# The opening of a diffusion backbone on one core: where the small rows load, who squares, and in which order tiles are turned

## The chip, the core and the metric

The kernel runs on one core of a Trainium2 chip. The metric is device time in microseconds (us); lower is better. The kernel before takes 922.6 us, the median of three runs (922.02, 922.60, 925.86).

A core has engines that run side by side and wait for each other by semaphores: TensorE (PE) multiplies matrices and turns tiles, VectorE (DVE) and ScalarE (ACT) work element by element, GpSimd (POOL) does the same slowly and starts loads, SyncE (SP) starts loads. PSUM is the memory that TensorE writes; its banks hold 128 x 512 floats each here.

## What is computed

One layer of a backbone on 512 latent tokens x and 256 context tokens, width 1024. The opening computes the modulation from c and the normed, modulated input, and starts the first products with `w_in`:

```
sh1x, sc1x, ... = split(silu(c) @ w_ada + b_ada, 6)       # for c and for c_ctx
hx = rms_norm(x, norm1_g) * (1 + sc1x) + sh1x
z = hx @ w_in                                              # 512 x 7200
u, vs, q, r, ga, gb, k, v, lr = split(z)
a = spatial_gating(gelu(u), gelu(vs))
o = gated linear attention over q, k, v, decay from lr, states started by the context tokens
y = (sigmoid(ga) * (a @ w_br_a) + sigmoid(gb) * (silu(r) * norm(o) @ w_br_b)) @ w_o
x = x + g1x * y
x = x + g2x * conv_glu(modulate(rms_norm(x, norm2_g)))
out = rms_norm(x, final_norm_g)
```

Products are taken in three parts: each operand is split in a high part (float32r, rounded) and a low part (the rest), and high*high, high*low and low*high are summed.

## The kernel before

x lies in four token tiles of 128 tokens, each in two halves of 512 columns (`xin[t][0]`, `xin[t][1]`). What the opening does, by line of the kernel before:

- POOL makes the identity, ones and two triangular masks (L105 to L117). ACT starts four small loads, `rows_a` (L127): c, c_ctx, norm1_g (8 rows of 128 each) and b_ada (48 rows), and `w_lr` (L314). POOL starts a second set of small rows and `w2r` (L350 to L357).
- SyncE starts the loads of x (eight of 256 KB, L134), then the ada weights in six groups (`ada_load`, L324) with the first weights of v, q and k between them (`first_load`, L330 and L333). These loads keep the order of the code. The framework gives each load started by SyncE or ACT one of eight lanes in turn; a load waits until the load before it on its lane has landed. Loads of POOL have lanes of their own.
- TensorE turns `rows_a` to columns (`columns`, L515, into `vec_a`), runs ten warm-up products of ones (L608; the trace shows each as two passes), then turns x: per tile seven blocks of 128 columns into seven banks (`xps`, L592).
- `norm_tiles` walks the tiles one at a time: ACT squares both halves with a sum (L546), small steps on VectorE and ACT make the root (L550 to L560), VectorE scales the tile (L563, L567; ACT scales the second half of the last one, L565), then `x_turns` turns it. Ahead of the last tile's turns stand the first ada dot (`ada_dot(0)`, L631: 32 small products), its copy by VectorE (L602) and its selection (`ada_sel`, L640, with three small steps on VectorE, L643 to L645).
- `ada_mod(0)` (L652) modulates the first block from its bank on ACT, VectorE casts the high part (L379) and takes the low part (L380). `first_high(0)` casts the first weights on ACT (L614), `x_out` copies the turned blocks out of their banks (L597). The eighth block is turned into a bank of the pool `mm` after that (`ps7`).
- The first products (`first_step`, L708) run over eight blocks k in three parts z, for q, k and four tiles of v (six products a part). The next ada group's dot, selection and modulation stand between them. The four v products use the four banks of the pool `mm`, so each waits until one is copied out.

TensorE, ACT and VectorE keep the order in which the code is recorded (`in_order` from `STRICT` on); what is recorded ahead of `STRICT` is ordered by the framework.

Of the kernel before, what the change touches and what calls it, by code (L numbers as in the profile page):

```python
# [11 lines left out]
U32 = mybir.dt.uint32  # L12
# [21 lines left out]
def backbone_kernel(  # L34
# [63 lines left out]
    def table_for(func):  # L98
# [9 lines left out]
    maskf = const([P, P], "maskf")  # L108
    G.affine_select(out=maskf, in_=ones, pattern=[[1, P]], base=0, channel_multiplier=-1,
                    compare_op=ALU.is_ge, fill=0.0)  # L110
    maskb = const([P, P], "maskb")
    G.affine_select(out=maskb, in_=ones, pattern=[[-1, P]], base=0, channel_multiplier=1,
                    compare_op=ALU.is_ge, fill=0.0)
# [4 lines left out]
    masks = (maskf.bitcast(U32), maskb.bitcast(U32))  # L118


# [5 lines left out]
    for o, ap in ((0, c[0]), (8, c_ctx), (16, norm1_g[0]), (24, b_ada[0])):  # L126
        adma(rows_a[o:o + ap.shape[0] // P, :], r8(ap))  # L127
# [186 lines left out]
    adma(w_lr, wi[:, O_LR:O_LR + 32].rearrange("(k p) c -> p k c", p=P))  # L314
# [13 lines left out]
    def first_load(i):  # L328
        rows = lambda c0, n: wi[2 * i * P:(2 * i + 2) * P, c0:c0 + n].rearrange("(k p) c -> p k c", p=P)
        dma(fv[i][0], rows(O_V, 512))  # L330
        raw = heap([P, 2, 2, P], s="qkraw")
        for j, c0 in enumerate((O_Q, O_K)):
            dma(raw[:, j], rows(c0, P))  # L333
        fqk.append((raw, late([P, 2, 2, P], F32R, s="qkh"), late([P, 2, 2, P], F32R, s="qkl")))
# [7 lines left out]
    was[4] = ada_load(4)  # L342
    first_load(2)
# [7 lines left out]
    G.dma_start(rows_b[32:40, :], gla_b2[0].rearrange("d (h p) -> (d h) p", p=P))  # L351
    w2r = []
# [160 lines left out]
    def columns(rows, n, name, bank=mm):  # L513
# [3 lines left out]
        V.tensor_copy(cols_, ps[:, :n])  # L517
        return cols_

    vec_a = columns(rows_a, 72, "vec_a")  # L520
    cT, n1g, bada = vec_a[:, 0:16], vec_a[:, 16:24], vec_a[:, 24:72]
    sg = small(16, "sg")
    A.activation(sg, cT, AF.Exp, scale=-1.0)
    V.tensor_scalar(sg, sg, 1.0, None, op0=ALU.add)
    V.reciprocal(sg, sg)
    cs = const([P, KT, 32], "cs")
    V.memset(cs, 0.0)
    V.tensor_tensor(cs[:, :, 0], cT[:, 0:8], sg[:, 0:8], op=ALU.mult)
    V.tensor_tensor(cs[:, :, 1], cT[:, 8:16], sg[:, 8:16], op=ALU.mult)
# [5 lines left out]
    bsc1 = const([P, 8], "bsc1")  # L535
    V.tensor_scalar(bsc1, bada[:, 8:16], 1.0, None, op0=ALU.add)
# [51 lines left out]
    STRICT = len(traced())  # L588
    xps = [(mm, gl)[k < 1 or k > 4]() for k in range(KT - 1)]
# [8 lines left out]

    def x_turns(t):
        if t == 3:  # L600
            dot0.extend(ada_dot(0))
            V.tensor_copy(*dot0)  # L602
            ada_sel(0, dot0[0])
# [1332 lines left out]
```

## Time and profile before

| | us |
|---|---|
| median of three runs | 922.6 |
| profiled execution, its own time | 921.73 |
| its span (first to last instruction) | 919.7 |
| VectorE, ACT and POOL busy in the span | 755.4, 484.7, 62.8 |
| TensorE busy from 0 to 22 us | 15.31 |
| loads started by SyncE, share of 16 DMA engines over the span | 41.0% |

The sums below are made against the profiled execution, which is 0.9 us faster than the median. In a row of the timeline stand the start, the duration, the engine, the line, the operation, the tile written and the tiles read, and in brackets how long the engine was idle before and what ended that. A row of stretches has the start and end, then the length, then busy time and number of instructions of PE, PEld (weight loads of TensorE), DVE, ACT and POOL, the granted clock, the DMA share and GB/s.

### The profile page before, as it was taken

What the parts mean: (1) busy time and instruction counts of PE and PEld (TensorE: products, weight loads), DVE (VectorE), ACT (ScalarE), POOL (GpSimd) and SP (SyncE); (2) the same over time, 40 slices, a digit from 0 to 9 for tenths busy, and PEclk for the clock granted to TensorE, in tenths of its full rate; (3) what the DMA queues carried; (4) which work ended last, traced back from release to release, by engine and by line L of the source; (5) the groups of instructions that cost most, each with busy time, mean ns of one, the idle gap of its engine ahead of it and who ended that gap; (6) DMA issues with size and microseconds to landing.
All of it is one profiled execution on the core that took longest, in us unless ns stands there. A gap on an engine that the chain in (4) does not pass through costs nothing.

```text
span 919.7 us, 12868 instructions
## 1 busy us (share of the span) xinstructions
PE 899.5 (98%) x4671; PEld 756.4 (82%) x4671; DVE 755.4 (82%) x1307; ACT 484.7 (53%) x869; POOL 62.8 (7%) x98
## 2 busy tenths in 40 slices
PE   7999999999999999999999998999999999999996
PEld 5777899988888888888888888988888888888885
DVE  5667686779589877978776887899998888899896
ACT  5156464657466447566552568543333443356673
POOL 3000000000000011113011010000000000122100
PEclk9999999999999999999999999999999999999998
DMA  9950512142088375978578164264444333399532
GB/s 275 338 159 1 154 31 59 34 115 70 15 279 306 97 202 124 288 171 219 160 206 206 33 175 138 69 178 131 126 131 133 104 91 115 79 231 260 151 92 92
DMA packets 125821, 134.27 MB, mean 146 GB/s; under 512 B 7178, under 2 KB 84310, under 8 KB 125758
## 3 DMA queue, kind: packets, MB, share of 16 engines
q1 hardware_dynamic: 115357, 116.80, 41.0%
q0 software_dynamic: 8672, 15.43, 10.3%
q10 hardware_dynamic: 1728, 1.22, 0.4%
q8 instruction: 37, 0.61, 0.3%
q14 instruction: 27, 0.21, 0.1%
HBM read 131.32 MB, written 2.10 MB: 145 GB/s over the span
## 4 chain that ended last, share of the span: by engine, by line
PE 89%; DVE 6%; ACT 2%; issue 1%; DMA 1%; ACTq 0%; DVEq 0%
PE mm L387 31%; PE mm L418 11%; PE gl L465 7%; PE gl L1719 6%; PE mm L465 5%; PE mm L1719 4%; PE gl L418 4%; PE gl L935 3%; PE mm L402 3%; PE mm L708 2%; PE mm L411 2%; PE gl L708 1%; PE mm L1041 1%; DVE mx L902 1%; PE gl L631 1%
## 5 line engine op out<-in xcount | busy, mean ns | idle before, releaser
L149 ACT CAST wh<-raw 128x1024 fp32r<-128x1024 f32 x110 | 115.0, 1050 | 113.4 <-PE mm L387 73.1
L150 DVE TENSOR_TENSOR wl<-raw,wh 128x1024 fp32r<-128x1024 f32 x110 | 133.6, 1220 | 34.2 <-ACT wh L149 31.7
L1602 DVE SCALAR_TENSOR_TENSOR cacc<-ca,ccol,cacc 128x441 f32<-128x441 f32 (+2 forms) x176 | 121.0, 693 | 6.7 <-ACT cacc L1590 3.6
L387 PE MATMUL mm<-h2l,wh 128*128 128x512 f32 x320 | 124.5, 389 | 0.0
L387 PE MATMUL mm<-h2h,wl 128*128 128x512 f32 x320 | 124.5, 389 | 0.0
L387 PE MATMUL mm<-h2h,wh 128*128 128x512 f32 x320 | 124.5, 389 | 0.0
L387 PEld LDWEIGHTS mm<-h2h,wl 128*128 128x128 f32 x320 | 60.1, 188 | 12.6
L387 PEld LDWEIGHTS mm<-h2l,wh 128*128 128x128 f32 x320 | 60.1, 188 | 12.5
L387 PEld LDWEIGHTS mm<-h2h,wh 128*128 128x128 f32 x320 | 60.1, 188 | 12.4
L1190 DVE SCALAR_TENSOR_TENSOR acc<-wa,cs,acc 128x512 f32<-128x512 f32 x64 | 45.8, 747 | 3.4 <-DMA wa<-in_w_ada_dram 3.4
L1605 ACT ACTIVATE cacc<-cacc 128x512 f32<-128x512 f32 x22 | 13.9, 632 | 60.6 <-DVE cacc L1602 60.5
L387 PE MATMUL mm<-hxh,wh 128*128 128x512 f32 x104 | 41.7, 401 | 0.0
L387 PE MATMUL mm<-hxh,wl 128*128 128x512 f32 x104 | 40.9, 394 | 0.0
L387 PE MATMUL mm<-hxl,wh 128*128 128x512 f32 x104 | 40.5, 390 | 0.0
L223 ACT CAST wh<-tt 128x512 fp32r<-128x512 f32 x48 | 28.3, 621 | 20.4 <-DMA tt<-in_w_in_dram 7.5
L224 DVE TENSOR_TENSOR wl<-tt,wh 128x512 fp32r<-128x512 f32 x48 | 31.6, 687 | 7.9 <-ACT wh L223 7.8
L1661 ACT CAST wh<-raw 128x1024 fp32r<-128x1024 f32 x22 | 23.0, 1052 | 18.2 <-PE mm L1719 9.0
L199 POOL DMA_DIRECT2D tt<-in_w_in_dram x24 | 20.8, 1064 | 165.5 <-DVE xl L1291 71.8
L1662 DVE TENSOR_TENSOR wl<-raw,wh 128x1024 fp32r<-128x1024 f32 x22 | 26.9, 1223 | 2.6 <-ACT wh L1661 2.6
L1641 POOL DMA_DIRECT2D b<-in_ffn_w_down_dram x11 | 9.4, 865 | 276.8 <-DMA b<-in_ffn_w_down_dram 268.3
L465 PE MATMUL mm<-wh,hxh 128*128 128x512 f32 x72 | 28.0, 389 | 0.0
L465 PE MATMUL mm<-wl,hxh 128*128 128x512 f32 x72 | 28.0, 389 | 0.0
(527 smaller groups left out, 2449.9 us busy)
## 6 DMA issues: line engine op xcount, KB each, us to landing
raw<-in_w_in_dram SPq DMA_DIRECT2D x54, 512.0 KB, 4.6
wa<-in_w_ada_dram SPq DMA_DIRECT2D x96, 256.0 KB, 5.0
raw<-in_ffn_w_up_dram SPq DMA_DIRECT2D x44, 512.0 KB, 3.9
raw<-in_ffn_w_down_dram SPq DMA_DIRECT2D x22, 512.0 KB, 3.3
tt<-in_w_in_dram POOLq DMA_DIRECT2D x24, 256.0 KB, 6.5
raw<-in_w_br_a_dram SPq DMA_DIRECT2D x8, 512.0 KB, 5.2
raw<-in_w_br_b_dram SPq DMA_DIRECT2D x8, 512.0 KB, 3.8
raw<-in_w_o_dram SPq DMA_DIRECT2D x8, 512.0 KB, 6.0
```

The lines of the kernel that those rows point to most:

```text
L149: A.copy(wh, raw)
L150: V.tensor_tensor(wl, raw, wh.bitcast(F32), op=ALU.subtract)
L223: A.copy(wh[:, kk, :], tt[j][kk])
L224: V.tensor_tensor(wl[:, kk, :], tt[j][kk], wh[:, kk, :].bitcast(F32), op=ALU.subtract)
L387: T.matmul(ps, a[:, k, :], b[:, c0:c0 + n], start=(k == 0 and i == 0), stop=(k == KT - 1 and i == 2))
L402: T.matmul(pss[u], a[:, k, :], b[:, c0:c0 + n], start=(k == 0 and z == 0), stop=(k == KT - 1 and z == 2))
L418: T.matmul(ps, a, b[:, k % 2, :], start=(k == 0 and i == 0), stop=(k == KT - 1 and i == 2))
L465: T.matmul(ps[t], a, b[:, kk, :], start=(first and i == 0), stop=(j == 1 and kk == 1 and i == 2), skip_group_check=again)
L708: T.matmul(fps[i], a, b, start=(k == 0 and z == 0), stop=(k == KT - 1 and z == 2))
L1190: V.scalar_tensor_tensor(a_, w_, cs[:, k, 0:1], a_, op0=ALU.mult, op1=ALU.add)
L1602: V.scalar_tensor_tensor(o, a_[:, r0 + dy:r1 + dy, c0 + dx:c1 + dx], wcol(tap), o, op0=ALU.mult, op1=ALU.add)
L1719: T.matmul(ps, a[:, t * P:(t + 1) * P], w[b][:, j, c0:c0 + n], start=(first and i == 0), stop=(last and i == 2), skip_group_check=again)
```

## The change

It touches the opening alone.

1. The four small loads of `rows_a` are started by POOL instead of ACT, ahead of the two masks. `w_lr` is loaded by SyncE, behind the fifth ada group. In `first_load` the q and k columns go ahead of the v columns.
2. `vec_a` is turned into a bank of the other pool (`gl`), and its copy is recorded later, behind the first root.
3. The squares of a tile's first half run on ACT, those of the second half on VectorE (`x_sq`). One root is taken for two tiles (`x_root`, `x_root_end`). First halves are scaled by VectorE (`x_low`), second halves by ACT (`x_high`).
4. Tiles 0 and 1 are turned whole, then the first four blocks of tiles 2 and 3, then the first ada dot, then the last three blocks of tiles 2 and 3, then the selection.
5. The scale `am` is made in one step with a column `bsn` prepared earlier. For the first block ACT writes the high part straight from the bank, and VectorE the full value from the bank and then the low part.
6. The eighth block is turned in the first products (k = 0, ahead of part z = 2) into a bank of `gl`. The cast of the first q and k weights stands ahead of the first modulation, that of v behind it and one copy.

```diff
-        adma(rows_a[o:o + ap.shape[0] // P, :], r8(ap))
+        G.dma_start(rows_a[o:o + ap.shape[0] // P, :], r8(ap))
...
-    adma(w_lr, wi[:, O_LR:O_LR + 32].rearrange("(k p) c -> p k c", p=P))
...
     was[4] = ada_load(4)
+    dma(w_lr, wi[:, O_LR:O_LR + 32].rearrange("(k p) c -> p k c", p=P))
...
-        V.tensor_tensor(am[:, ks, :], sv[:, :, 1, :], bsc1[:, ks].unsqueeze(2).to_broadcast([P, ng, 2]), op=ALU.add)
-        V.tensor_tensor(am[:, ks, :], am[:, ks, :], n1g[:, ks].unsqueeze(2).to_broadcast([P, ng, 2]), op=ALU.mult)
+        for b in range(ng):
+            k = k0 + b
+            V.scalar_tensor_tensor(am[:, k, :], sv[:, b, 1, :], n1g[:, k:k + 1],
+                                   bsn[:, k:k + 1].to_broadcast([P, 2]), op0=ALU.mult, op1=ALU.add)
...
-                A.activation(f, xps[0], AF.Identity, bias=bm_[:, 0, 0:1], scale=am[:, 0, 0:1])
+                A.activation(hi, xps[0], AF.Identity, bias=bm_[:, 0, 0:1], scale=am[:, 0, 0:1])
+                V.tensor_scalar(f, xps[0], am[:, 0, 0:1], bm_[:, 0, 0:1], op0=ALU.mult, op1=ALU.add)
+                V.tensor_tensor(lo, f, hi.bitcast(F32), op=ALU.subtract)
...
+    def x_sq(t, ss):
+        for hf in range(2):
+            junk = heap([P, 512], BF16, s="junk")
+            if hf == 0:
+                A.activation(junk, xin[t][0], AF.Square, accum_out=ss[:, t % 2:t % 2 + 1])
+            else:
+                V.scalar_tensor_tensor(junk, xin[t][1], 1.0, xin[t][1], op0=ALU.mult, op1=ALU.mult,
+                                       accum_out=ss[:, 2 + t % 2:3 + t % 2])
...
+    for t in range(2):
+        x_sq(t, ssx[0])
+    root0 = x_root(ssx[0])
+    x_root_end(*root0)
+    vec_copy[0]()
+    A.activation(sg, cT, AF.Exp, scale=-1.0)
+    for t in range(2):
+        x_low(t, root0[1])
+    x_sq(2, ssx[1])
+    x_high(0, root0[1])
...
+    x_sq(3, ssx[1])
+    x_high(1, root0[1])
+    root1 = x_root(ssx[1])
...
+    for t in range(2):
+        for k in range(KT - 1):
+            x_turn(xps[k], t, k)
+    for t in range(2, 4):
+        for k in range(4):
+            x_turn(xps[k], t, k)
     x_out(1, xps[1], V.tensor_copy)
+    dst, aps = ada_dot(0)
+    V.tensor_copy(dst, aps)
+    for t in range(2, 4):
+        for k in range(4, KT - 1):
+            x_turn(xps[k], t, k)
+    ada_sel(0, dst)
+    A.copy(*fqk[0][1::-1])
     ada_mod(0)
...
+            if k == 0 and z == 2:
+                ps7 = gl()
+                for t in range(4):
+                    x_turn(ps7, t, KT - 1)
+                x_out(KT - 1, ps7, A.copy)
```

Three places in the order of instructions. First POOL's queue at its start; `rows_92` and `rows_88` are `rows_a` before and after, `rows_223` and `rows_219` the second set. Before, POOL goes from the identity to the masks and then to the second set (`rows_a` is in ACT's queue):

```order
masks.py:199 AFFINE_SELECT ident<-ident 128x128
L109 AFFINE_SELECT maskf<-ones 128x128
L112 AFFINE_SELECT maskb<-ones 128x128
L115 MEMSET eps_t 128x1
L117 MEMSET one_t 128x1
L350 DMA rows_223<-in_norm_g_dram 8x128
L350 DMA rows_223<-in_sgu_ln_g_dram 8x128
```

And now:

```order
masks.py:199 AFFINE_SELECT ident<-ident 128x128
L109 MEMSET eps_t 128x1
L111 MEMSET one_t 128x1
L118 DMA rows_88<-in_c_dram 8x128
L118 DMA rows_88<-in_c_ctx_dram 8x128
L118 DMA rows_88<-in_norm_g_dram 8x128
L118 DMA rows_88<-in_b_ada_dram 48x128
L344 AFFINE_SELECT maskf<-ones 128x128
L347 AFFINE_SELECT maskb<-ones 128x128
L341 DMA rows_219<-in_norm_g_dram 8x128
```

The four small loads stand in POOL's queue where the masks stood, and b_ada is the last of them as before.

Second, ACT between the scaling of the last x tile and the first copies; `xT` are turned blocks, `qkh` and `wh` the high parts of the first weights. Before:

```order
L565 ACTIVATE xin_110<-xin_110,r_363 128x512
L652 ACTIVATE xT_270<-gl_263,bm,am 128x512
L614 CAST qkh_139<-qkraw_136 128x512
L614 CAST wh_114<-raw_113 128x1024
L597 COPY xT_273<-mm_266 128x512
L597 COPY xT_274<-mm_267 128x512
L597 COPY xT_277<-mm_425 128x512
```

And now:

```order
L772 ACTIVATE xin_102<-xin_102,r_107_325 128x512
L772 ACTIVATE xin_106<-xin_106,r_107_325 128x512
L811 CAST qkh_134<-qkraw_130 128x512
L645 ACTIVATE hxh_393<-gl_257,bm,am 128x512
L595 COPY xT_267<-mm_260 128x512
L815 CAST wh_110<-raw_109 128x1024
L595 COPY xT_268<-mm_261 128x512
```

The cast of the q and k weights moved ahead of the modulation, which now writes the high part `hxh`; the copy of the eighth block (`xT_277` from `mm_425`) is gone from this stretch.

Third, TensorE behind the first block's dot. The eighth block's turns (into `mm_425` before, `gl_453` now) read `xin`; `gl_436` and `gl_407` are the bank of q. Before:

```order
L592 MATMUL gl_269<-ident,xin_110 128x128
L592 MATMUL mm_425<-ident,xin_98 128x128
L592 MATMUL mm_425<-ident,xin_102 128x128
L592 MATMUL mm_425<-ident,xin_106 128x128
L592 MATMUL mm_425<-ident,xin_110 128x128
L708 MATMUL gl_436<-hxh_416,qkh_139 128x512
```

And now, after the second group's selection:

```order
L630 MATMUL gl_444<-selm,asb_438 128x4
L590 MATMUL gl_453<-ident,xin_94 128x128
L590 MATMUL gl_453<-ident,xin_98 128x128
L590 MATMUL gl_453<-ident,xin_102 128x128
L590 MATMUL gl_453<-ident,xin_106 128x128
L704 MATMUL gl_407<-hxh_393,qkl_135 128x512
```

The four turns moved from ahead of the first product to between the second and the third part of the first block's products.

More of the change, by code (lines that the diff above doesn't have):

```diff
@@ L107, in backbone_kernel @@
     G.memset(ones, 1.0)
[L108 to L113, printed above, removed]
     eps_t = const([P, 1], "eps_t")
@@ L333, in first_load @@
             dma(raw[:, j], rows(c0, P))
+        dma(fv[i][0], rows(O_V, 512))
         fqk.append((raw, late([P, 2, 2, P], F32R, s="qkh"), late([P, 2, 2, P], F32R, s="qkl")))
@@ L351, in backbone_kernel @@
     G.dma_start(rows_b[32:40, :], gla_b2[0].rearrange("d (h p) -> (d h) p", p=P))
+    maskf = const([P, P], "maskf")
+    G.affine_select(out=maskf, in_=ones, pattern=[[1, P]], base=0, channel_multiplier=-1,
+                    compare_op=ALU.is_ge, fill=0.0)
+    maskb = const([P, P], "maskb")
+    G.affine_select(out=maskb, in_=ones, pattern=[[-1, P]], base=0, channel_multiplier=1,
+                    compare_op=ALU.is_ge, fill=0.0)
+    masks = (maskf.bitcast(U32), maskb.bitcast(U32))
     w2r = []
@@ L510, in rstd_of, with columns @@
         return r
-    def columns(rows, n, name, bank=mm):
+    def columns(rows, n, name, bank=mm, then=None):
         ps = bank()
@@ L516, in columns @@
         cols_ = const([P, n], name)
-        V.tensor_copy(cols_, ps[:, :n])
-        return cols_
[L520 to L525, printed above, removed]
+        copy = lambda: V.tensor_copy(cols_, ps[:, :n])
+        if then is None:
+            copy()
+        else:
+            then.append(copy)
+        return cols_
     cs = const([P, KT, 32], "cs")
     V.memset(cs, 0.0)
-    V.tensor_tensor(cs[:, :, 0], cT[:, 0:8], sg[:, 0:8], op=ALU.mult)
-    V.tensor_tensor(cs[:, :, 1], cT[:, 8:16], sg[:, 8:16], op=ALU.mult)
     selm = const([P, 4], "selm")
@@ L588, in backbone_kernel @@
     STRICT = len(traced())
+    vec_copy = []
+    vec_a = columns(rows_a, 72, "vec_a", gl, vec_copy)
+    cT, n1g, bada = vec_a[:, 0:16], vec_a[:, 16:24], vec_a[:, 24:72]
+    sg = small(16, "sg")
+    bsc1, bsn = const([P, 8], "bsc1"), const([P, 8], "bsn")
     xps = [(mm, gl)[k < 1 or k > 4]() for k in range(KT - 1)]
@@ L597, in x_out @@
         eng(fx[k], ps)
[L599 to L603, printed above, removed]
-        for k in range(KT - 1):
-            x_turn(xps[k], t, k)
     for i in range(10):
@@ new lines, in x_low, with x_high @@
+    def x_low(t, r):
+        V.tensor_scalar(xin[t][0], xin[t][0], r[:, t % 2:t % 2 + 1], None, op0=ALU.mult)
+    def x_high(t, r):
+        A.mul(xin[t][1], xin[t][1], r[:, t % 2:t % 2 + 1])
+    ssx = [small(4, "ssx") for _ in range(2)]
+    for t in range(2):
[8 more added lines that the diff above has]
+    x_high(0, root0[1])
@@ L756, in backbone_kernel @@
+    first_low(0)
     x_out(4, xps[4], A.copy)
-    ps7 = mm()
-    for t in range(4):
-        x_turn(ps7, t, KT - 1)
-    x_out(KT - 1, ps7, A.copy)
+    x_out(5, xps[5], A.copy)
     x_out(6, xps[6], V.tensor_copy)
-    first_low(0)
-    x_out(5, xps[5], A.copy)
     lrx = heap([96, S], F32R, s="lrx")
```

37 lines of the change are left out of this document (28 added, 9 removed).

## The prediction

> **What bounds the kernel now.** I read the page first, then TensorE's waits, its timeline over the first 22 us, and the chain of waits over the same stretch. The page says which engine carries the span.
>
> ```profile
> span 919.7 us, 12868 instructions
> PE 899.5 (98%) x4671; PEld 756.4 (82%) x4671; DVE 755.4 (82%) x1307; ACT 484.7 (53%) x869; POOL 62.8 (7%) x98
> PE 89%; DVE 6%; ACT 2%; issue 1%; DMA 1%; ACTq 0%; DVEq 0%
> ```
>
> TensorE is busy 98% of the span and holds 89% of the chain that ended last. The order view shows differences in the opening alone, and the number of TensorE rows is the same. So the question is how much sooner or later TensorE gets through its opening. The busy time by stretches says where that can matter at all:
>
> ```profile
> 0.00:22.00 22.00, 15.31 (x127) 11.78 (x127) 13.36 (x54) 12.60 (x34) 8.15 (x24) 1.00 1.01 274
> 22.00:64.00 42.00, 42.00 (x303) 30.50 (x295) 24.97 (x64) 11.23 (x24) 1.00 (x2) 1.00 0.90 267
> ```
>
> From 22 to 64 us TensorE has no idle time (42.00 of 42.00). Only the first 22 us, with 6.7 us idle, can give or take anything; whatever shift stands at 22 us is carried on. The waits of TensorE in the first 80 us, all of them:
>
> ```profile
> PE mm L515 <- DMA rows<-in_b_ada_dram: 5.8, 1, 5.8
> PE gl L640 <- DVE asb L602: 0.4, 1, 0.4
> PE mm L592 <- DVE xT L597: 0.3, 1, 0.3
> PE gl L708 <- ACT qkh L614: 0.2, 1, 0.2
> ```
>
> 5.8 of them is one wait: for the last of the four small row loads. No wait is for an x tile or an ada weight. The timeline of TensorE shows what hangs on that load (start, duration, last in brackets the idle time before it):
>
> ```profile
> 5.80 0.35 PE L515 MATMUL mm<-ident,rows 72*128 72x72 f32 x1 [5.80 <-DMA rows<-in_b_ada_dram]
> 5.95 6.34 PE L608 MATMUL mm<-ident,ones 128*128 128x256 f32 x20
> 12.13 0.27 PE L592 MATMUL gl<-ident,xin 128*128 128x128 f32 x1
> ...
> 14.51 1.08 PE L631 MATMUL gl<-wa,cs 128*32 128x128 f32 x32
> 16.01 0.39 PE L640 MATMUL gl<-selm,asb 128*128 128x4 f32 x2 [0.41 <-DVE asb L602]
> ...
> 18.34 0.70 PE L708 MATMUL gl<-hxh,qkh 128*128 128x512 f32 x2 [0.18 <-ACT qkh L614]
> ...
> 21.13 1.08 PE L631 MATMUL gl<-wa,cs 128*32 128x128 f32 x32
> ```
>
> TensorE's queue is in order: turn the rows, 20 warm-up passes (6.2 us, to 12.13), 21 turns of x (2.4 us), the first ada dot, its selection, the first product at 18.34. The first x tile is ready well before 12.13, when VectorE's scaling of its second half ends:
>
> ```profile
> 10.14 0.48 DVE L567 TENSOR_SCALAR xin<-xin,r 128x512 f32<-128x512 f32 x1
> ```
>
> The chain of waits (start, us, what) begins its part of TensorE with that load as well:
>
> ```profile
> 2.12 3.55 DMA rows<-in_b_ada_dram
> 5.67 0.14 issue
> ```
>
> So the opening is bound by **the landing of the small rows plus TensorE's own queue**, not by norms or lanes.
>
> **The change, part by part.** *Small rows on POOL.* How POOL's small loads run now:
>
> ```profile
> 1.51 0.29 POOL L109 TENSOR_SCALAR_AFFINE_SELECT maskf<-ones 128x128 f32<-128x128 f32 x1
> 1.99 0.09 POOL L115 MEMSET eps_t<- 128x1 f32 x1
> 2.07 0.68 POOL L350 DMA_DIRECT2D rows<-in_norm_g_dram  x1
> 3.79 0.52 POOL L350 DMA_DIRECT2D rows<-in_gla_norm_g_dram  x1
> DMA to landing us min/median/max: 3.6/3.7/4.2
> ```
>
> Without the two masks (1.51 to 1.99) POOL's first load starts at 2.07-0.48 = 1.59. The last of the four, b_ada, starts where the fourth does now: 1.59+(3.79-2.07) = 3.31. Landing takes 3.6 to 4.2 us for 4 KB; b_ada has 24 KB, so I take 3.9: it lands at 7.2, and its turn on TensorE starts 0.14 later (the issue row above), at 7.35. Against 5.80 that is **+1.55**. Bounds: 3.2 us, the landing of an x load, gives 6.5 and +0.85; 5.0 us, POOL's 32 KB w2r loads in the first 50 us, gives 8.3 and +2.65:
>
> ```profile
> xin<-in_x_dram SPq DMA_DIRECT2D x8, 256.0 KB, 3.2
> w2r<-in_gla_w_dram POOLq DMA_DIRECT2D x6, 32.0 KB, 5.0
> ```
>
> Behind the four loads on POOL stand the masks, the second set of rows and w2r. The second set starts some 2.3 us later than at 2.07 and is first used by its turn on TensorE, far behind: hidden.
>
> ```profile
> 36.03 0.25 PE L515 MATMUL gl<-ident,rows 40*128 40x40 f32 x1
> ```
>
>
> *SyncE's lanes.* SyncE now waits 2.7 us for lanes among the x loads. What its loads moved meanwhile:
>
> ```profile
> SPq L134 <- DMA xin<-in_x_dram: 2.7, 2, 1.7
> 2.00:6.00 4.00, 0.20 (x2) 0.23 (x2) 0.23 (x3) 0.08 (x1) 2.82 (x8) 1.00 0.93 299
> ```
>
> 299 GB/s and a busy share of 0.93 with those waits in it: the transfers nearly fill the DMA engines already, and freed lanes bring at most 7% of 4 us, 0.3 us. TensorE waits for none of these loads, so I take 0. The Trainium skill ("DMA: Bandwidth & Descriptors", section "Issuing engines are not separate DMA queues") says that loads begun on several engines run on the same 16 DMA engines and that spreading them saves only issue time. By it the lanes are worth 0 too and the move to POOL as well; the trace agrees for the lanes. w_lr goes behind five ada groups, and the q and k columns ahead of v: earlier or equal for what the opening needs. Ahead of w_lr stand then 2 MB of x, 6 MB of five ada groups and 1.5 MB of first weights; 9.5 MB at 299 GB/s from 2 us on make 34, and its first reader stands on TensorE behind the turn at 36.03: hidden.
>
> *Squares on two engines, roots for two tiles.* A square with an accumulator on VectorE is not in the trace. Nearest is its pass with two operands over 128x512; the two rows below it are the first and the last step of a root on VectorE:
>
> ```profile
> L1190 DVE SCALAR_TENSOR_TENSOR acc<-wa,cs,acc 128x512 f32<-128x512 f32 x64 | 45.8, 747 | 3.4 <-DMA wa<-in_w_ada_dram 3.4
> 7.93 0.16 DVE L550 TENSOR_TENSOR ss<-ss 128x1 f32<-128x1 f32 x1 [0.47 <-ACT junk L546]
> 9.26 0.16 DVE L560 SCALAR_TENSOR_TENSOR r<-t,r 128x1 f32<-128x1 f32 x1
> ```
>
> I take 0.75; bounds 0.48 (the scaling above) and 1.5 (twice the pass). With 2 MB of x at 299 GB/s from 2 us the eighth tile is there at 9.0 and the fourth at 5.5. VectorE then goes: square to 6.3, root 1.5 (as 7.93 to 9.42 now) to 7.8, vec_a behind the rows to 7.9, two scalings to 8.8, square, 0.8 of small work and square to 11.1, root to 12.6, scalings to 13.5. TensorE wants those at about 15.2 (13.7 when the shifted warm-up ends, plus 14 turns of 0.11). The gain in the norms is real and **hidden: 0**; the cover is 1.7 us, and at 1.2 a square (+0.45 for each of the last three in this chain, 1.4) it still holds.
>
> *Turns before the dot, selection, high part from the bank.* 22 turns ahead of the dot instead of 21: +0.1. Six turns (0.65) behind it where TensorE now waits 0.41 for the copy: selection +0.2. From selection to first product it is 2.33 now. Two steps of VectorE on that way go, the second am step and the cast to the high part, and the qk cast, for which TensorE waited 0.2 at the end, now stands ahead of ACT's modulation:
>
> ```profile
> 16.62 0.16 DVE L644 TENSOR_TENSOR am<-am,vec_a 128x2 f32<-128x2 f32 x1
> 17.77 0.43 DVE L379 CAST hxh<-xT 128x512 fp32r<-128x512 f32 x1 [0.32 <-ACT xT L652]
> PEld mm L708 <- ACT xT L597: 0.6, 2, 0.3
> ```
>
> 0.16+0.43+0.14 (from the end of the cast at 18.20 to 18.34) is **-0.7**; 1.6 remain. Between 18.34 and 21.13 the four v products waited twice for copies by ACT (0.6 in all, last row) because the eighth tile held one of their banks; it now goes to another: I take -0.3, between 0 and -0.6. That eighth tile's four turns now lie free in a wait of TensorE ahead of 18.34 (0.3 of it for VectorE's xT); in the change they stand between products: 4 of 0.11, +0.45.
>
> Sum: 1.55+0.1+0.2-0.7-0.3+0.45 = **+1.3 us**. The profiled execution took 921.73 (span 919.7 and 2.0 around it): 923.0. The median of the runs shown is 0.9 higher, 922.6, which gives 923.9. I say **923.4**.
>
> **Rivals.** *Neutral, or a hair faster:* the rows land on POOL in 3.2 us, as an x load does (1.55 becomes 0.85), and the warm-up passes change pace at the same time as now although they start later (-0.8, next rival). For it: POOL's queue holds nothing else then. Against: no small POOL load in the trace landed in under 3.6. Then 1.3-0.7-0.8 = -0.2: 921.5 to 922.4.
>
> *The warm-up runs slow for longer.* Passes of L608 early and late (min, median, max ns, first and last start):
>
> ```profile
> L608 PE MATMUL mm<-ident,ones x8: 634/634/729, 6.0 to 9.0; 128*128 128x256 f32 x8
> L608 PE MATMUL mm<-ident,ones x12: 379/379/457, 9.5 to 11.9; 128*128 128x256 f32 x12
> ```
>
> They start 0.43 apart before 9.5 and 0.22 after. 20 slow ones would take 8.6 us, 20 fast ones 4.4, against 6.2. If the change of pace keeps its distance from the first pass, nothing is added; if the shifted start makes it come late, up to +2.4, if it comes at the same 9.5, -0.8. I price the late case at +1.5 on top: 924.9. What decides is whether the pace changes more than 3.6 us after the first pass. The Trainium skill ("TensorE: Matmul & The Clock Gate", Part 1) says that a free-running window of about 3.4 us of activity sets the clock, so that the turn comes 3.4 us or more after the start depending on the phase; the rows agree with that (3.6 us), and by it this term scatters from run to run.
>
> *Slower by over 0.5%:* the rows land so late that TensorE, and with it VectorE at vec_a, stands still. Each us costs one us; 4.6 us is reached 3.3 us behind the forecast's landing, at 10.5, 7.2 us after issue. Nearest against it: 5.0 for 32 KB. It would give 926.4 or more on the profiled execution's base, 927.2 on the median's.
>
> *The part doesn't do what it says:* VectorE's squares cost 1.5 or more and the turns wait for x instead: 924 to 926.
>
> **How the numbers follow.** Forecast 0.52, neutral 0.22, slow warm-up 0.18, norms late 0.04, rows very late 0.04. The range reaches from the neutral case, less the early pace (921.7-0.8 = 920.9), to the late pace with the higher base and rows at their upper bound (924.9+1.1 = 926.0): 920.8 to 926.0. 0.5% is 4.6 us, about what a measurement of this kernel tells from no change; of the cases only the last lies beyond it on the slow side, none on the fast side: faster 0.01, same 0.95, slower 0.04.
>
> **What would show it.** TensorE's first wait grows from 5.8 to 7.3 (6.6 to 8.5) and still names rows of b_ada; the first turn of x starts at about 13.7; VectorE's last scaling ends before TensorE asks for it; from selection to first product 1.6 instead of 2.33; the first product near 19.4 and the second ada dot near 22. I am wrong if the rows land by 6, if TensorE waits for xin, wa or qkraw in the opening, or if the shift at 22 us isn't found again at the end.

## The result and the profile after

The changed kernel is slower: 928.16 us median (926.24 to 931.05, 7 runs) beside 923.22 us (7 runs) of the kernel before, a ratio of 1.0051 with a 95% interval of 1.0032 to 1.0070. Timed a second time, beside variants of itself (e9 below), it took 927.49 us beside 923.20, a ratio of 1.0042 (1.0027 to 1.0057). The price is 4 to 5 us. The forecast was 923.4 us with a range up to 926.0, so the time lies outside it. The span of the profiled execution grew by 4.7 us, from 919.7 to 924.4. TensorE's last product starts at 914.95 instead of 910.43, 4.5 us later, and the table below has 4.3 us at 27.64, so the loss of the opening is carried to the end, as the forecast said.

The busy time by stretches of the kernel after has the same columns as before. From 26 us on TensorE has no idle time up to 64 us:

```profile
0.00:22.00 22.00, 11.51 (x86) 9.51 (x86) 11.39 (x46) 10.62 (x23) 10.30 (x28) 1.00 1.01 270
22.00:26.00 4.00, 4.00 (x38) 2.79 (x38) 2.82 (x4) 0.71 (x2) 0.00 (x0) 0.57 1.15 312
26.00:64.00 38.00, 38.00 (x284) 28.10 (x277) 21.95 (x50) 8.80 (x18) 0.99 (x2) 1.00 0.91 264
```

In the first 22 us TensorE is busy for 11.51 us instead of 15.31. The row from 22 to 26 us shows something that the kernel before did not have in its opening: a granted clock of 0.57 while TensorE is busy all the time. (Much later, near 560 us, both kernels have such a stretch.) The waits of TensorE in the first 30 us, all of them:

```profile
PE gl L513 <- DMA rows<-in_b_ada_dram: 8.7, 1, 8.7
PE gl L704 <- ACT hxh L645: 1.2, 1, 1.2
PE gl L704 <- DVE xT L646: 0.3, 1, 0.3
PE gl L704 <- DVE hxl L647: 0.2, 1, 0.2
```

The first is the same load as before, now 2.9 us later. The other three are new, and all stand ahead of the first products. TensorE's timeline at those places (start, duration, in brackets the idle time ahead):

```profile
18.90 0.28 PE L630 MATMUL gl<-selm,asb 128*128 128x4 f32 x2
20.37 0.50 PE L704 MATMUL gl<-hxh,qkh 128*128 128x512 f32 x1 [1.19 <-ACT hxh L645]
21.22 0.50 PE L704 MATMUL gl<-hxh,qkh 128*128 128x512 f32 x1 [0.34 <-DVE xT L646]
21.95 1.18 PE L704 MATMUL gl<-hxl,qkh 128*128 128x512 f32 x2 [0.22 <-DVE hxl L647]
22.92 1.91 PE L704 MATMUL mm<-wh,hxh 128*128 128x512 f32 x4
24.76 1.39 PE L621 MATMUL gl<-wa,cs 128*32 128x128 f32 x32
...
27.64 0.71 PE L704 MATMUL gl<-hxh,qkl 128*128 128x512 f32 x2
```

Set against the kernel before, the delay goes like this (starts that are in no row above are read from the same two timelines):

| TensorE starts | before | after | later by |
|---|---|---|---|
| turn of the rows | 5.80 | 8.73 | 2.93 |
| first turn of x | 12.13 | 14.68 | 2.55 |
| first ada dot | 14.51 | 17.18 | 2.67 |
| selection | 16.01 | 18.90 | 2.89 |
| first product | 18.34 | 20.37 | 2.03 |
| first product with x's low part | 18.98 | 21.95 | 2.97 |
| second ada dot | 21.13 | 24.76 | 3.63 |
| first product with the weights' low part | 23.31 | 27.64 | 4.33 |

So there are two pieces: some 2.9 us that come in with the rows and stand again at the selection (the warm-up was 0.4 shorter, turns and selection 0.3 later), and some 1.4 us that are added behind the selection. The first product did come forward, by 0.86 against the selection, but at the products with x's low part that was gone. The chain of waits has the first piece in two rows (start, us, what):

```profile
1.63 1.71 POOL rows L118 x3
3.34 5.26 DMA rows<-in_b_ada_dram
```

POOL issued the last load at 3.34, as forecast (3.31). It landed 5.26 us later, not 3.9. The DMA issues in the first 30 us (KB each, median us from issue to landing) show that it is not alone:

```profile
xin<-in_x_dram SPq DMA_DIRECT2D x8, 256.0 KB, 5.3
...
rows<-in_b_ada_dram POOLq DMA_DIRECT2D x1, 24.0 KB, 5.3
rows<-in_c_dram POOLq DMA_DIRECT2D x1, 4.0 KB, 3.9
rows<-in_c_ctx_dram POOLq DMA_DIRECT2D x1, 4.0 KB, 4.6
rows<-in_sgu_ln_g_dram POOLq DMA_DIRECT2D x1, 4.0 KB, 6.2
```

The loads of 4 KB on POOL's queue land 3.9 to 6.4 us after issue, most of the later ones more slowly, while before the change loads of this kind took 3.6 to 4.2. The figure for x must be read with care: the profile tells the landing of one load of x alone, the second one before (3.2) and the sixth one now (5.3), so it does not say that the same load became slower. What did change is how fast SyncE starts its eight loads of x, before and after:

```profile
0.81 6.15 SPq L134 DMA_DIRECT2D xin<-in_x_dram  x8
```

```profile
0.81 3.70 SPq L125 DMA_DIRECT2D xin<-in_x_dram  x8
```

Before, SyncE stopped after four of them until a lane was free. Now it does not stop, and six have been started when POOL starts the last row at 3.34.

### The profile page after: what moved, and what is told of

The parts are those of the page before. It is cut to its first block, busy times and chain, and to the rows that moved or that the text cites. A ratio compares the mean times of both kernels' runs of the same rounds, so it can differ in the third digit from the quotient of the medians.

```text
span 924.4 us, 12852 instructions
## 1 busy us (share of the span) xinstructions
PE 900.1 (97%) x4671; PEld 757.5 (82%) x4671; DVE 755.7 (82%) x1299; ACT 484.3 (52%) x860; POOL 64.8 (7%) x102
## 4 chain that ended last, share of the span: by engine, by line
PE 93%; DVE 3%; ACT 1%; issue 1%; DMA 1%; POOL 0%; ACTq 0%; POOLq 0%
PE mm L385 31%; PE mm L416 11%; PE gl L463 9%; PE mm L463 7%; PE gl L1780 6%; PE mm L1780 4%; PE gl L416 4%; PE gl L996 3%; PE mm L400 3%; PE mm L704 2%; PE mm L409 2%; PE gl L704 1%; PE mm L1102 1%; PE gl L621 1%; DVE mx L963 1%; PE gl L1029 1%
```

## The experiments

Three theories. **A**: the rows hold TensorE's opening, and they are late because SyncE, freed of its lane waits, now puts six loads of x ahead of the last of them where it stopped at four. **B**: the idle time of TensorE ahead of the first products halves its clock for the following 3.4 us. **C**: the high part from the bank brings the first product forward and nothing behind it. The rival to all of them is that the loss lies elsewhere (other loads, norms, the order of the weights).

All times stand beside the kernel before, measured in the same set: 923.80 us beside e1 to e4, 924.31 beside e5 to e8, 923.20 beside e9 to e12. Runs of different sets are therefore compared by their ratios:

| run | what differs from the kernel after | median us | ratio to before (95%) |
|---|---|---|---|
| e1 | rows on ScalarE's queue | 925.02 | 1.0020 (1.0007 to 1.0032) |
| e2 | four lanes taken | 924.59 | 1.0018 (1.0003 to 1.0032) |
| e3 | kernel before, rows on POOL | 925.97 | 1.0037 (1.0020 to 1.0054) |
| e4 | eighth tile's turns in the gap | 928.46 | 1.0062 (1.0047 to 1.0077) |
| e5 | filling products | 926.83 | 1.0029 (1.0015 to 1.0043) |
| e6 | warm-up ahead of the rows | 926.59 | 1.0026 (1.0012 to 1.0041) |
| e7 | first block as before | 926.76 | 1.0026 (1.0011 to 1.0040) |
| e8 | e1 and e5 | 923.53 | 0.9992 (0.9979 to 1.0005) |
| e9 | nothing | 927.49 | 1.0042 (1.0027 to 1.0057) |
| e10 | e1, longer filling, first block as before | 924.06 | 1.0010 (0.9998 to 1.0022) |
| e11 | e1, six turns behind the selection | 923.90 | 1.0002 (0.9988 to 1.0015) |
| e12 | e11, first block as before | 923.40 | 1.0000 (0.9991 to 1.0009) |

### e1: the rows back on ScalarE's queue

```diff
-        G.dma_start(rows_a[o:o + ap.shape[0] // P, :], r8(ap))
+        adma(rows_a[o:o + ap.shape[0] // P, :], r8(ap))
```

> The kernel after, with one part undone: the four loads of the small rows (L118) are issued by ScalarE's queue again and not by POOL; everything else stays. Theory A (the late rows hold TensorE's opening and carry most of the loss): the turn of the rows (L513) starts at about 5.8 us instead of 8.73, the ten warm-up products end near 12 instead of 14.68, then the scaled tiles 2 and 3 set the pace (ready at 14.65 and 15.1 in the kernel after, and x itself lands no earlier), so the first ada dot starts at 15.0 to 15.5 instead of 17.18, and the span is 2 to 2.5 us shorter: 922.0 to 922.5. Rival (what the loss comes from lies behind the first dot: the first products and the half clock at 22.03 to 25.44): the rows are early, but the span stays within 0.7 us of 924.4.

The rows were turned at 6.17, the first dot started at 15.16, and the ratio fell from 1.0042 to 1.0051 down to 1.0020: some 2 to 3 us are back, as theory A says. The span of the profiled execution, 923.2, was 0.7 above the expected range; at 267 us TensorE was 2.0 us ahead of the kernel after, as expected, and 1 us of it was lost again later (the end of the part on the prediction has more on this). Its clock dropped as in the kernel after. The rows below are stretches of 3.4 us, the first around the wait for the first products, the second behind it; the third number from the end is the granted clock:

```profile
17.15:20.56 3.41, 1.66 (x6) 0.92 (x6) 2.47 (x6) 3.03 (x5) 0.99 (x3) 1.00 1.22 291
20.56:23.97 3.41, 3.41 (x37) 2.25 (x35) 2.25 (x3) 0.14 (x1) 0.00 (x0) 0.50 1.22 285
```

What is left over the kernel before, 0.2%, was then the question for theory B.

### e2: four lanes taken

```diff
+    spare = const([32, P], "spare")
+    for o in range(0, 32, 8):
+        adma(spare[o:o + 8, :], r8(c[0]))
```

> The kernel after, with four loads of 4 KB added on ScalarE's queue at its start, into a tile that nothing reads (extra work, no part of the result). They take four of the eight lanes that SyncE's loads also use, so that SyncE again has only four loads of x outstanding; the rows stay on POOL. Theory A (each small row lands when the x load that was issued just before it lands: 5.55, 6.88, 7.24 and 8.59 us stand beside x loads at 6.07, 7.05, 7.72 and 8.41 that were issued at 1.71, 2.18, 2.65 and 3.13): with only four x loads ahead the last row lands 3.6 to 4.2 us after its issue at 3.34, at 7.0 to 7.6, L513 starts there, and the first dot is 0.8 to 1.3 us earlier than 17.18. Rival (loads that POOL issues at this time are late whatever stands in SyncE's queue): the last row still lands at 8.4 to 8.8 and nothing moves. By theory A the span is 923.2 to 923.8, by the rival 924.4 or, with the added loads in the way, some tenths more.

Four loads that nothing needs made the kernel faster than the kernel after. They hold SyncE back again, and the rows land sooner. SyncE's loads of x, and the DMA issues:

```profile
0.81 5.44 SPq L128 DMA_DIRECT2D xin<-in_x_dram  x8
```

```profile
rows<-in_b_ada_dram POOLq DMA_DIRECT2D x1, 24.0 KB, 3.6
```

The last row was issued at 3.33, landed at 6.97, 3.6 us later instead of 5.3, and was turned at 7.10, with POOL's instructions where they were. That is theory A's number and excludes the rival that POOL's loads are slow at this time by themselves. The first dot came 0.56 earlier, less than expected, because the warm-up took 6.9 us instead of 5.8 in this execution; the ratio is as good as that of e1. The span, 922.3, was below the expected range: the clock also stayed at 1.00 in this execution (in the stretch around the gap TensorE was busy for 2.18 of 3.4 us, against 1.66 in e1), so part of this gain belongs to theory B. SyncE's lane waits, which the forecast priced at 0, had kept the x loads out of the rows' way. The Trainium skill ("DMA: Bandwidth & Descriptors", section "Queues, rings and completion order") says that each DMA engine takes packets from its queues in turn and that a load's completion mark on an engine is written only after all earlier writes of that engine, whichever queue they came from. The landing times agree with it; the runs show no more than these times.

### e3: the kernel before with its rows on POOL

```diff
-        adma(rows_a[o:o + ap.shape[0] // P, :], r8(ap))
...
+        G.dma_start(rows_a[o:o + ap.shape[0] // P, :], r8(ap))
```

(The four loads stand ahead of the masks, as in the kernel after.)

> The kernel before, with one part of the change alone: the four loads of the small rows are issued by POOL ahead of its masks and not by ScalarE, so that SyncE no longer waits for lanes among the loads of x. Theory A (depth of SyncE's queue): the last row lands at 8.2 to 8.8 us instead of 5.67, the turn of the rows (L515 there) starts as late, the warm-up ends at 14.4 to 15.0 instead of 12.13, the first product starts 2.3 to 2.9 us later than 18.34, and the span is 2.2 to 2.9 us longer than 919.7: 921.9 to 922.6; the rest of the 4.7 us is then owed to the other parts. Rival 1 (the forecast's own price): the rows land 3.9 us after their issue at 3.3, the span is 920.9 to 921.3. Rival 2 (the late rows are hidden by the other waits): within 0.5 us of 919.7.

```profile
8.43 0.35 PE L516 MATMUL mm<-ident,rows 72*128 72x72 f32 x1 [8.43 <-DMA rows<-in_b_ada_dram]
8.58 6.92 PE L609 MATMUL mm<-ident,ones 128*128 128x256 f32 x20
```

Alone, this edit of the change moves the turn of the rows from 5.80 to 8.43 (expected 8.2 to 8.8). The first product starts at 21.55, 3.2 us later and not 2.3 to 2.9; 0.6 of it is a longer warm-up. The median is 0.37% above before: most of the price of the whole change. The span, 925.4, is above the expected range (921.9 to 922.6): of the 5.7 us to before, 3.1 stand at 268 us, and the rest came later, partly through a wait of 1.1 us near 410 us that this execution had and that of before had not.

### e4: the eighth tile's turns in the gap

The four turns of the eighth tile and their copy (`ps7`, `x_turn(ps7, t, KT - 1)`, `x_out`) are recorded ahead of the first products instead of inside them.

> The kernel after, with the four turns of the eighth tile (0.39 us) put back between the selection and the first products, where TensorE waits 1.19 us, instead of behind the low parts. Theory B (TensorE's idle time ahead of the first products halves its clock: in the 3.4 us from 18.61 to 22.03 it was busy for 1.66 us, and the clock granted from 22.03 to 25.44 was 0.50, while the kernel before was busy for 2.95 us in the like stretch and kept 1.00): with the turns it is busy for 2.0 to 2.3 us there; if that is enough, the clock stays at 1.00, the second ada dot starts at 23.9 to 24.3 instead of 24.76, the eighth tile's turns no longer stand among the products later, and the span is 1.3 to 2.2 us shorter: 922.2 to 923.1. Rival (the drop hangs on something else, or more than two thirds of the stretch have to be busy): the clock is 0.50 again, only the 0.39 us are saved or nothing, span 923.9 to 924.4.

A miss: the span grew to 926.7 and the clock dropped. TensorE waited more, not less:

```profile
PE gl L704 <- ACT xT L595: 1.0, 1, 1.0
PE gl L704 <- DVE xT L646: 0.9, 1, 0.9
PE gl L590 <- DVE bm L637: 0.5, 1, 0.5
```

The turns took the bank that the first product of q had used, so q and k had to wait for two other banks of the same pool to be read out. TensorE was busy for only 1.15 of the 3.4 us there instead of the 2.0 to 2.3 that were meant, so the drop agrees with theory B but decides nothing between it and its rival. What it does show is that the four banks of that pool are all in use at this place.

### e5: products that only fill the gap

```diff
     ada_sel(0, dst)
+    for i in range(4):
+        T.matmul(xps[1][:, :256], ones, ident.unsqueeze(1).to_broadcast([P, 2, P]), start=True, stop=True)
     A.copy(*fqk[0][1::-1])
```

> The kernel after, with four more products of the warm-up's kind (ones by the identity, 256 columns, into the bank that the second tile has just left; extra work, no part of the result) between the selection and the first products, where TensorE waits 1.19 us. Theory B (TensorE's own idle time ahead of the first products halves its clock for the next 3.4 us): it is then busy for 2.7 to 2.9 us of the 3.4 us in which it was busy for 1.66, the granted clock stays at 1.00 through the first products, and from the first product to the first product with the low part of the weights (20.37 to 27.64, 7.27 us, in the kernel after) it takes 5.7 to 6.0 us, as in the run with the lanes taken (19.81 to 25.56, 5.75 us), where the clock happened to stay at 1.00. The median falls by 1.0 to 1.7 us from 928.16. Rival (the drop comes from the warm-up's end or the time since it, not from the hole): the clock is 0.50 there again, the stretch takes 7.2 to 7.5 us, the median does not move.

```profile
19.31:22.72 3.41, 3.18 (x16) 2.25 (x15) 2.23 (x5) 2.79 (x5) 1.24 (x3) 1.00 1.23 292
22.72:26.13 3.41, 3.41 (x45) 2.54 (x43) 2.70 (x5) 0.39 (x1) 0.00 (x0) 1.00 1.13 304
```

TensorE was busy for 3.18 of 3.41 us and the clock stayed at 1.00. From the first product (21.05) to the first one with the weights' low part (26.50) it took 5.45 us against 7.27, less than the 5.7 to 6.0 expected. The first product came 0.3 us later behind the selection than in the kernel after, so the fair count is from the selection (19.29) on: 7.21 us against 8.74. The ratio, 1.0029, is 0.0022 below the first and 0.0013 below the second timing of the kernel after (2.0 and 1.2 us), and the intervals overlap: the mechanism is shown by the trace, its size in the median is not settled by this pair alone.

### e6: the warm-up ahead of the rows

```diff
+    warm = mm()
+    for i in range(10):
+        T.matmul(warm[:, :256], ones, ident.unsqueeze(1).to_broadcast([P, 2, P]), start=True, stop=True)
     vec_a = columns(rows_a, 72, "vec_a", gl, vec_copy)
```

(The ten products behind it are gone, and `warm` serves as `xps[1]`.)

> The kernel after, with the ten warm-up products ahead of the turn of the rows instead of behind it. Theory A (TensorE's opening hangs on the rows because the turn of the rows stands first in its queue): the warm-up starts at 1.6 to 1.9 us and is over by 7.5 to 9, the rows are turned when they land (8.4 to 8.7), the first turn of x starts when tile 0 is scaled, at 9.8 to 10.2 instead of 14.68, the turns of tiles 2 and 3 wait for their norm (13.9 to 15.1), and the first dot starts at 15.0 to 15.5 instead of 17.18; TensorE is idle between the turns of tiles 1 and 2, so that its clock may drop there, which would give back up to 1.5 us. The median is 925.0 to 927.0, against 928.16. Rival (the opening is held by the loads or the norms as well): the first dot stays at 16.5 or later, and the median within 0.7 us of 928.2.

The first dot started at 15.03, as expected (17.18 in the kernel after), so the rows in TensorE's queue had held it. What holds it now is the norm of the third tile:

```profile
14.00 0.33 PE L593 MATMUL gl<-ident,xin 128*128 128x128 f32 x1 [1.66 <-DVE xin L770]
```

What theory B had warned of came too. Stretches behind each other:

```profile
12.47:15.88 3.42, 1.88 (x40) 1.67 (x40) 2.22 (x7) 1.79 (x5) 0.14 (x1) 1.00 1.13 293
15.88:19.30 3.41, 1.88 (x19) 1.28 (x10) 1.64 (x5) 2.41 (x4) 1.83 (x4) 1.00 1.22 289
19.30:22.71 3.41, 3.30 (x11) 1.88 (x14) 3.38 (x5) 1.27 (x3) 0.00 (x0) 0.50 1.21 273
```

TensorE was busy for 1.88 us in two stretches, and only behind the second did the clock drop. The median, 926.59, lies in the expected range; the ratio, 1.0026, is above e1's.

### e7: the first block modulated as before

```diff
-                A.activation(hi, xps[0], AF.Identity, bias=bm_[:, 0, 0:1], scale=am[:, 0, 0:1])
-                V.tensor_scalar(f, xps[0], am[:, 0, 0:1], bm_[:, 0, 0:1], op0=ALU.mult, op1=ALU.add)
-                V.tensor_tensor(lo, f, hi.bitcast(F32), op=ALU.subtract)
...
+                A.activation(f, xps[0], AF.Identity, bias=bm_[:, 0, 0:1], scale=am[:, 0, 0:1])
```

> The kernel after, with the first block modulated as before: ScalarE writes the full value from the bank, VectorE casts the high part and takes the low. Theory C (the high part written straight from the bank brings the first products forward but not the low part, since VectorE reads the bank only when ScalarE has done, 19.54 to 20.22 and then 20.36 to 21.17): the first product starts 2.1 to 2.4 us behind the selection instead of 1.47, but the products with the low part start 2.9 to 3.2 us behind it, as now (3.05), and the median stays within 0.7 us of 928.2. Rival (the direct high part is worth its 0.86 us all the way): the low products and the median come 0.7 to 1.0 us later.

The first product started 2.03 us behind the selection, the products with x's low part 2.67 behind it, against 3.05 with the change. So theory C was too kind to the change: the direct high part costs 0.4 us at that point. The two rows of the kernel after that show why, ScalarE's and VectorE's timeline:

```profile
19.54 0.78 ACT L645 ACTIVATE hxh<-gl,bm,am 128x512 fp32r<-128x512 f32 x1 [1.01 <-DVE bm L637]
```

```profile
20.36 0.81 DVE L646 TENSOR_SCALAR xT<-gl,am,bm 128x512 f32<-128x512 f32 x1 [0.85 <-ACT hxh L645]
21.20 0.69 DVE L647 TENSOR_TENSOR hxl<-xT,hxh 128x512 fp32r<-128x512 f32 x1
```

VectorE has what it needs for L646 at 19.5 but reads the bank only when ScalarE has read it: 0.85 us idle. The second product then waits for that same bank (0.34 in the list of waits). The Trainium skill ("PSUM — Partial Sum Buffer", section "PSUM bank collisions raise a hardware error") says that two engines must not access one bank at once, reads by both included; the trace agrees in that the program keeps them apart, and no run here lets them collide. The median was 1.4 us below the first timing of the kernel after, outside the 0.7 that was expected, and the ratio, 1.0026, is 0.0016 below e9's with intervals that overlap; the clock did not drop in this profile, and how often it does with one long gap in place of three short ones wasn't settled.

### e8: the rows on ScalarE's queue and the filling products

> The kernel after, with two edits: the small rows on ScalarE's queue again, and the four filling products between the selection and the first products. If A and B are the two causes and add up: the rows are turned at 5.7 to 6.2 us, the clock stays at 1.00 through the first products, and the median is 923.2 to 924.0 (925.02 of the run with the rows alone, less 1.0 to 1.7), within 0.2% of the kernel before. If the clock is not a cause: 924.7 to 925.4.

The two edits together bring 923.53 us, 0.9992 of before, in the expected range; e1 alone left 1.0020. TensorE's timeline has the rows at 5.84, and the norms as the next limit:

```profile
13.92 0.33 PE L590 MATMUL gl<-ident,xin 128*128 128x128 f32 x1 [0.43 <-DVE xin L769]
...
14.94 1.08 PE L621 MATMUL gl<-wa,cs 128*32 128x128 f32 x32
```

The chain of waits leads from that norm back to a load of x, issued at 5.92 (4.07 in the kernel after) because the rows on ScalarE's queue take lanes again:

```profile
5.92 5.17 DMA xin<-in_x_dram
```

The first dot still starts 0.43 later than before the change. With early rows the norms, and the last load of x behind them, are no longer hidden; the change put the dot behind turns of all four tiles, where the kernel before had it behind three.

### e9: the kernel after again

> The kernel after, unchanged, so that it is timed beside variants of itself and gives a second profile. If the price of the change holds, the median is again 0.3 to 0.7% above the kernel before (925 to 931 us); the rows land at 8.2 to 8.9. If the run with the first block as before (926.76, 0.26% above) was no faster than the kernel after, and the two only differ by the days they were measured on, this median lies at 926.5 to 927.2.

The price holds. This profile paid it in another way: the rows landed 6.0 us after their issue, at 9.32 and later than the 8.2 to 8.9 expected, were turned at 9.46, and the warm-up took 7.28 us. But the gap fell across two stretches, and the clock stayed:

```profile
18.91:22.32 3.41, 2.48 (x45) 2.02 (x43) 1.27 (x4) 1.20 (x2) 1.93 (x4) 1.00 1.22 290
22.32:25.74 3.42, 2.60 (x8) 1.42 (x8) 3.15 (x5) 2.60 (x5) 0.03 (x1) 1.00 1.15 311
```

From the selection (21.10) to the first product with the weights' low part (28.32) it took 7.22 us; 8.74 in the first profile of the same program, 7.30 in the kernel before. So the drop costs 1.5 us where it happens, and without it this part of the change is worth nothing either way (0.1 us).

### e10, e11, e12: real work in the gap, and the first block as before

e10 is e8 with six filling products instead of four and e7's edit. e11 is e1 with this edit, and e12 adds e7's:

```diff
-    for t in range(2, 4):
-        for k in range(4, KT - 1):
-            x_turn(xps[k], t, k)
     ada_sel(0, dst)
+    for t in range(2, 4):
+        for k in range(4, KT - 1):
+            x_turn(xps[k], t, k)
```

> The kernel after with three edits: small rows on ScalarE's queue, six filling products between the selection and the first products, and the first block modulated as before. In the runs whose clock held, the stretch from the selection to the first product with the weights' low part was 6.84 us with the first block as before (20.44 to 27.28), 7.22 us with the direct high part (18.34 to 25.56 and 16.67 to 23.89). Theory C2 (the bank that two engines read one after the other, and the second product that waits for that bank, cost 0.4 us more than the direct high part brings): the stretch is 6.7 to 6.9 us, and the median 0.2 to 0.6 us below that of the run with two edits (0.9992 of before), 0.9986 to 0.9990. Rival (the two ways are worth the same): stretch 7.1 to 7.3, ratio 0.9988 to 0.9996.

> The kernel after with two edits: small rows on ScalarE's queue, and the six turns of tiles 2 and 3 (columns 4 to 6 of the blocks) put behind the selection, where they stood before; no filling products. Theory B: the turns take 0.65 us of the 1.19 us hole, but TensorE now waits 0.4 to 0.5 us for the copy ahead of the selection, as in the kernel before; the selection is 0.2 to 0.3 us earlier, the stretches of 3.4 us hold 0.9 to 1.2 us of idle time, less than in the run with the lanes taken (1.23, clock kept), so the clock stays at 1.00 and the median is 922.8 to 923.8 of 924.0 before (0.9985 to 1.0000). Rival (moving real work in does not spare the clock): 0.50 again in the stretch behind the first products, ratio 1.0015 to 1.0025 like the run with the rows alone.

> The kernel after with three edits: small rows on ScalarE's queue, the six turns of tiles 2 and 3 behind the selection, and the first block modulated as before. TensorE is idle for about 1.1 us in one piece ahead of the first products and for 0.4 ahead of the selection. If theories B and C2 both hold: clock kept, from the selection to the first product with the weights' low part 6.7 to 6.9 us, and the median 0.9980 to 0.9996 of before, the best of all; if only B holds, like the run without the third edit.

e10 missed: the six products held TensorE until 19.33, so that the first product came 2.63 us behind the selection (2.03 in e7); the stretch took 7.33 us (16.70 to 24.03), longer than theory and rival had it, and the ratio was 1.0010. e11 met theory B: the turns shortened the wait for ScalarE from 1.19 to 0.48 us,

```profile
16.73 0.31 PE L590 MATMUL mm<-ident,xin 128*128 128x128 f32 x1
...
18.05 0.50 PE L704 MATMUL gl<-hxh,qkh 128*128 128x512 f32 x1 [0.48 <-ACT hxh L645]
```

the clock stayed at 1.00 and the ratio went from e1's 1.0020 to 1.0002 (0.9985 to 1.0000 was expected). e12's stretch was 6.94 us (17.35 to 24.29) against e11's 7.33 (16.48 to 23.81), the 0.4 us of e7 again; its median, 1.0000 of before and above the 0.9980 to 0.9996 expected, can't be told from e11's. No version here beats the kernel before by more than its interval.

## Why the prediction was wrong

- **Landing of the rows: the failing step.** "I take 3.9: it lands at 7.2" with an upper bound of 5.0. It landed 5.26 us (profile after) and 6.0 us (e9) after issue, and the term was 2.9 to 3.7 us instead of 1.55. The landing was taken from POOL loads of the kernel before, which ran while SyncE was held to four loads of x. The same change that moved the rows removed that hold. The lower bound, "the landing of an x load", rested on a single load, the second of x.
- **SyncE's lanes, priced at 0: the same mistake from the other side.** The argument looked at what x would gain (nothing, as e9 and the first profile confirm: TensorE waits for no x load) and not at who stood behind x. e2 shows it: with four lanes taken again the row lands after 3.6 us. So the sentence "the lanes are worth 0 too and the move to POOL as well" did not hold here: together they cost 2 to 3 us.
- **Norms hidden: right** for the kernel after, where VectorE's last scaling ended at 14.65 (forecast 13.5), ahead of TensorE's turns of these tiles, the first of which came at 16.2; but only because the rows were late. In e8 they are the next wait, 0.43 us, and in e6 1.66. The forecast had the eighth load of x at 9.0; in e8 it was there at 11.1.
- **Selection to first product, -0.7: right at its place (-0.86), wrong in what follows.** The two reads of one bank in L645 and L646 stand one behind the other, so the products with x's low part are no earlier; e7 and e12 put the loss against the old way at 0.4 us. The turns ahead of the dot (+0.1) and the selection (+0.2) came as priced, 0.12 and 0.22.
- **The four v products, -0.3, and the eighth tile, +0.45.** The turns cost their 0.39 (27.25 to 27.64 in the timeline). The gain at the v products can't be seen beside the lower clock; where the clock stayed (e9), the whole stretch behind the selection came out 0.1 shorter than before.
- **Not foreseen: the clock behind the gap.** Before, eleven turns stood between the selection and the first product (16.25 to 18.2 in the timeline); the change moved seven of them ahead of the selection and four behind the first parts. The forecast counted these moves at +0.2 and +0.45 of turns and put the hole that they leave at nothing, although it weighed the same 3.4-us window for the warm-up. It costs 1.5 us in an execution where it strikes; filling the hole brought e1 from 1.0020 to 1.0002 (e11, real work) and 0.9992 (e8, filling).
- **The rivals.** The slow warm-up came in e9 (7.28 us) and not in the first profile (5.8). The rows never landed as late as 10.5. The squares cost 0.69 and 0.08 us, as assumed. The lower end of the range, 920.8, took the early pace off from 921.7, a figure that is no case of the list (the neutral case is 921.5 to 922.4 with the early pace in it); it did not matter.

Together, by the medians: late rows some 2 to 3.5 us (e1, e2 and e3), the hole behind the selection some 1.5 to 2.5 (e11 and e8 against e1, and the stretches of e5 and e9), the rest about 0. The intervals of the medians, about 1.4 us to each side, allow no finer split, but the profiles do. A product far behind the opening, the first one of `swT` and `vsn`, starts at 265.07 us in the kernel before:

```profile
265.07 1.05 PE L1235 MATMUL gl<-swT,vsn 128*128 128x128 f32 x8
```

```profile
269.26 1.05 PE L1296 MATMUL gl<-swT,vsn 128*128 128x128 f32 x8
```

The second row is the kernel after. The table has how much later this product starts than before, how much of that is a longer or shorter warm-up (from its first pass to the first turn of x, 6.18 us before), and what is left:

| profile | later than before | by the warm-up | left |
|---|---|---|---|
| after | 4.19 | -0.38 | 4.57 |
| e9, the same program, clock kept | 4.92 | 1.10 | 3.82 |
| e1 | 2.18 | 0.17 | 2.01 |
| e11 | 0.39 | 0.05 | 0.34 |
| e12 | 0.88 | 0.98 | -0.10 |

Early rows take off 2.6 us (after to e1), the filled hole 1.7 (e1 to e11), the first block as before 0.4 (e11 to e12), and nothing is left. These are single executions, one each. Their spans do not show it so plainly, because behind this place the profiles part again, in all versions: between 390 and 480 us TensorE falls back by 1.9 us more in e3, by 1 in e1, and not at all in the profile after, and the half-clock stretch near 560 us is missing in e2, e8, e9, e10 and e11. So e8's span, 919.0, is no gain of the opening; its product above starts 0.44 us later than before.

Not tried: whether rows issued first on SyncE's own queue would land by 6 without holding x.

## What to carry to other kernels

A wait for a lane or a slot may be what keeps a long transfer from standing in front of a short one that everything hangs on: before removing it, list what is issued behind it, and take landing times only from loads that had as much in flight ahead of them. Work that is moved forward leaves a hole where it stood; if TensorE is idle for about half of a 3.4-us stretch there, price the next stretch at half clock, as these runs had it. Compare profiles at a place just behind the change, and not by their spans alone. A gain at the first product counts only if the second operand, and the bank of the second product, come as early.

## What the runs showed of the hardware

- **The clock drops after a half-idle stretch.** The clock records of the fourteen profiles change only at steps of 3.413 us. Cut into such stretches, counted from the first full clock and without the last twelve us of a run, where TensorE's work ends, nine stretches ran at full clock and had TensorE busy for 1.51 us or less: the next one ran at 0.50 each time. Of ten with 1.53 to 1.88 us, four did, so there the busy time alone does not decide. From 2.18 us on none did. Eight of the nine lie near 560 us, where TensorE waits in every version, the kernel before included; the ninth is e4's gap. The first profile after lies in the middle:

```profile
18.61:22.03 3.42, 1.66 (x10) 0.94 (x7) 1.93 (x6) 2.49 (x4) 1.44 (x3) 1.00 1.22 290
22.03:25.44 3.41, 3.41 (x22) 2.33 (x26) 2.79 (x4) 0.69 (x2) 0.00 (x0) 0.50 1.16 308
```

  The Trainium skill ("TensorE: Matmul & The Clock Gate", section "What's actually happening") names an idle window of about 3.4 us as the cause of a drop; here half of one was enough. e9, the same program with the stretches cut elsewhere, kept its clock.
- **The warm-up varies by 1.5 us.** The clock became full 2.9 to 5.9 us after the first warm-up product in the fourteen profiles, so at times earlier than the 3.4 us or more that the prediction took for it, and the same ten products (two passes each) took 5.8 to 7.3 us (e6 aside, where other work stands behind them). Minimum, median and maximum ns of a pass in the kernel after, first and second profile:

```profile
L598 PE MATMUL mm<-ident,ones x20: 379/379/728, 8.9 to 14.5; 128*128 128x256 f32 x20
```

```profile
L598 PE MATMUL mm<-ident,ones x20: 379/634/729, 9.6 to 16.7; 128*128 128x256 f32 x20
```

  This is likely a part of the spread of single executions (920.53 to 925.99 us for the kernel before in the last set), and a reason to compare medians and not the spans of two profiles. How much of that spread it makes is not shown.
